# Seven products in one more column group, the last columns moved forward, and a counted order for VectorE

## Chip, core and metric

The kernel runs on one core of a Trainium2 chip. The metric is the device time of one execution in microseconds. In the text PE is TensorE (matmuls), DVE VectorE, ACT ScalarE, POOL GpSimd, and SP the engine that issues most loads.

## What is computed

A two-layer encoder trunk on 256 tokens of width 1024, all in float32. A layer is a feed-forward block, an attention block and a second feed-forward block; a norm ends it all. The change lies in the four feed-forward blocks:

```python
def rms_norm(x, g):
    y = x * lax.rsqrt(jnp.mean(x * x, axis=-1, keepdims=True) + RMS_EPS)
    return y * g
def swiglu(h, w_gate, w_up, w_down):          # 1024 -> 2816 -> 1024
    return (jax.nn.silu(h @ w_gate) * (h @ w_up)) @ w_down
for l in range(2):
    x = x + 0.5 * swiglu(rms_norm(x, ffn1_norm[l]), ffn1_w_gate[l], ffn1_w_up[l], ffn1_w_down[l])
    x = x + attention(rms_norm(x, mix_norm[l]))   # w_in, two kinds of heads, w_out
    x = x + 0.5 * swiglu(rms_norm(x, ffn2_norm[l]), ffn2_w_gate[l], ffn2_w_up[l], ffn2_w_down[l])
return rms_norm(x, final_norm)
```

## The kernel before

**Splitting.** Each float32 operand is cut in two parts of the matmul type: ACT copies it into a rounded high part and DVE subtracts that from it to get the low part. A product is then three matmuls (high by high, low by high, high by low). All weights pass once through this: a step's weights (1 MB, 512 rows by 512 columns as 128 x 4 x 512) are loaded from memory into one of six buffers called raw by a DMA that SP issues, and split in two halves (`emit_split`), each into two of the 28 slots of the pool s4. A half costs one ACT copy and one DVE subtraction of 128 x 1024. Activations are kept turned (width on the partitions), split in the same way.

**Groups of columns.** A feed-forward block's 2816 inner columns are taken in groups: 0 to 4 of 512 columns, and the last 256, here called E. In a plain group gate and up are four steps of 24 matmuls each (four chunks of 128 rows, two halves of the tokens, three matmuls). The hidden values h = silu(gate) * up are then turned on PE (eight 128 x 128 transposes) and split (`turn`), and the down projection of that group, two steps of 24 matmuls named d0.0 and d0.1 for group 0, runs one group later, into four accumulators that stay in PSUM through the block.

**Seven products.** For the groups in `SEVEN` (2, 3, 4) gate and up are one 2 x 2 block product: tokens in two halves, rows in two halves, gate and up side by side. `by_seven` makes it of seven block products of 12 matmuls each instead of eight, in the order m1, m7, p2, p3, d0, p5, p6, p4, d1 (the two down steps of the group before lie in between). Their operands are sums. On the side of the activations four sums are made once a block (`make_sums`): each is a DVE operation, an ACT copy and a DVE subtraction, from float32 copies of the normed input (`copies`, eight ACT operations). On the side of the weights (`seven`): m1 takes block a, m7 takes b+c, p2 takes d, p3 takes c, p5 takes a+b, p6 takes a+b+c, p4 takes a+b+c+d. b+c and a+b are made by accumulating DMAs that POOL issues (`gather`), once the raw buffer below is loaded, for a also split; the other two by DVE additions into raw (`plus`, two of 128 x 1024 each). DVE then combines the seven products (seven operations of 128 x 512) and multiplies gate and up (`up`, twice).

**What sets the order.** In the feed-forward blocks each engine runs its instructions in the order in which the program writes them (`keep_in_program_order`). `weights()` gives PE the next step and calls `ahead`, which writes splits up to `look` halves further on; when PE gets to the second half of a step, `part` calls it once more. `look` is 8 in a block, is brought down to 7 and 6 in groups 3 and 4 (6 throughout in the first block), and is 6 elsewhere. `ahead` also writes loads, in the order of the steps, up to ten steps on and while fewer than six raw buffers are taken; the gather of c into b goes out right behind the load of b. The block's norm statistics are written in `before(2)`, after the splits up to step 5: DVE sums, POOL's power that gives r, and DVE again. Silu needs r.

**Order of a block.** Group 0, group 1 (plain, the sums in between), groups 2 to 4 by seven, E, and the end: d4.0 with the turn of E inside, E's own down step (dE), d4.1, the residual additions (`res.add`) and the transposes for the next norm (`pair`). `attention_constants` (first block) and `final_gain` (last block) come after E. The functions that the change touches, with what calls them:

## Time and profile before

| | us |
|---|---|
| median of three runs (935.18 to 935.84) | 935.23 |
| the profiled execution: its time, and the span that the profile covers | 935.0, 933.2 |
| PE busy, matmuls / weight loads | 921.1 / 780.7 |
| DVE, ACT, POOL busy | 759.9, 566.8, 55.0 |
| granted PE clock, mean over the span | 0.999 |
| HBM read | 192.71 MB, 208 GB/s |

Matmuls are pipelined: the profile's mean duration of one (392 ns for 512 columns) is longer than the distance from one to the next. DVE's and ACT's instructions overlap a little as well, so that the distance from start to start is shorter than the duration listed. Blocks are named first to fourth feed-forward here; the second and third stand directly behind each other, and an attention block lies between first and second, and between third and fourth. The first begins at 6.14 us, group 1 of the four at 30.84, 314.08, 492.31 and 771.83.

### The profile page before, as it was taken

Reading aid. Unit: us, or ns where it says so; the run is one execution under the profiler, and the core shown is the slowest. Engines: PE = TensorE matmul, PEld = TensorE weight load, DVE = VectorE, ACT = ScalarE, POOL = GpSimd, SP = SyncE. Lnnn points to the kernel's source line nnn. Section 1 sums busy time; section 2 is a strip of 40 time slices with the busy share of each in tenths; the row PEclk is TensorE's granted clock in tenths of the full one; section 3 lists DMA queues with packets and bytes.
Section 4 is the critical chain, followed back from the end, with each engine's and each line's share of the span. In section 5 each row is a group of like instructions: output and inputs, shape, how many; then the busy total and the mean of one; then the engine's idle time right before and its main releaser. Section 6 shows DMA issues by size and latency. Waiting matters only on the chain.

```text
span 933.2 us, 12665 instructions
## 1 busy us (share of the span) xinstructions
PE 921.1 (99%) x4796; PEld 780.7 (84%) x4796; DVE 759.9 (81%) x1074; ACT 566.8 (61%) x889; POOL 55.0 (6%) x73
## 2 busy tenths in 40 slices
PE   8999999999999999999999999999999999999997
PEld 6888878799898888888888888888999888888886
DVE  6759999869866588999776799996697566799994
ACT  7837576457745657576475466565577476466561
POOL 0400000000000001000000000000000000001011
PEclk9999999999999999999999999999999999999999
DMA  9996898827335858797767597887462367597831
GB/s 334 347 233 200 251 271 270 235 97 217 131 93 178 271 135 261 191 269 271 240 236 204 140 299 203 238 283 218 144 187 91 136 213 198 145 299 203 248 113 46
DMA packets 110893, 194.58 MB, mean 208 GB/s; under 512 B 3566, under 2 KB 31280, under 8 KB 110832
## 3 DMA queue, kind: packets, MB, share of 16 engines
q1 hardware_dynamic: 96528, 166.74, 52.8%
q0 software_dynamic: 12928, 25.46, 15.4%
q10 hardware_dynamic: 1376, 1.57, 0.5%
q8 instruction: 37, 0.61, 0.3%
q14 instruction: 24, 0.20, 0.1%
HBM read 192.71 MB, written 1.05 MB: 208 GB/s over the span
## 4 chain that ended last, share of the span: by engine, by line
PE 93%; DVE 4%; issue 1%; DMA 0%; ACT 0%; POOLq 0%; POOL 0%; ACTq 0%; DVEq 0%
PE ps L50 93%; DVE w L50 3%; DVE s L50 1%; DMA xk<-in_x_dram 0%; DVE tmp L50 0%; DVE raw L50 0%; ACT w L50 0%; DVE distA L50 0%; DVE xk L50 0%; DVE distB L50 0%; POOLq L1060 0%; POOL rf L50 0%; ACTq L50 0%; DVE lsum L50 0%; DVEq L50 0%
## 5 line engine op out<-in xcount | busy, mean ns | idle before, releaser
L50 PE MATMUL ps<-w,s 128*128 128x512 f32 (+1 forms) x2754 | 641.3, 391 | 1.2 <-DVE s L50 1.1
L50 PEld LDWEIGHTS ps<-w,s 128*128 128x128 f32 x2754 | 511.3, 188 | 107.5 <-DVE s L50 1.6
L50 DVE TENSOR_TENSOR w<-raw,w 128x1024 fp32r<-128x1024 f32 (+1 forms) x440 | 460.4, 1093 | 59.3 <-ACT w L50 58.1
L50 ACT CAST w<-raw 128x1024 fp32r<-128x1024 f32 (+1 forms) x440 | 391.1, 948 | 91.9 <-DVE raw L50 69.6
L50 PE MATMUL ps<-w,q 128*128 128x512 f32 x432 | 101.9, 389 | 0.0
L50 PEld LDWEIGHTS ps<-w,q 128*128 128x128 f32 x432 | 81.1, 188 | 16.8
L50 PE MATMUL ps<-s,w 128*128 128x256 f32 x672 | 84.0, 285 | 0.0
L50 PEld LDWEIGHTS ps<-s,w 128*128 128x128 f32 x672 | 81.7, 191 | 1.1
L50 ACT ACTIVATE s<-ps,gcol 128x256 fp32r<-128x256 f32 (+1 forms) x80 | 31.5, 488 | 47.0 <-PE ps L50 47.0
L50 DVE TENSOR_TENSOR raw<-raw,raw 128x1024 f32<-128x1024 f32 x48 | 56.5, 1219 | 0.0
L50 ACT CAST s<-ps 128x512 fp32r<-128x512 f32 x48 | 26.1, 593 | 46.5 <-PE ps L50 46.5
L50 POOL DMA_DIRECT2D raw<-in_ffn_w_up_dram x24 | 31.1, 1296 | 352.9 <-DVE w L50 166.5
L50 DVE TENSOR_TENSOR s<-ps,s 128x512 fp32r<-128x512 f32 x48 | 31.0, 684 | 25.1 <-ACT s L50 25.1
L50 PE MATMUL ps<-ident,s 128*128 128x128 f32 x304 | 39.9, 274 | 0.6 <-DVE s L50 0.6
L50 PEld LDWEIGHTS ps<-ident,s 128*128 128x128 f32 x304 | 35.0, 141 | 5.9 <-DVE s L50 1.4
L50 ACT ACTIVATE tmp<-tmp,r 128x512 f32<-128x512 f32 x24 | 17.3, 722 | 34.0 <-DVE tmp L50 34.0
L50 ACT ACTIVATE s<-s,negm 128x256 f32<-128x256 f32 x64 | 31.9, 500 | 6.3 <-DVE negm L50 6.1
L50 PE MATMUL ps<-w,v 128*128 128x512 f32 x144 | 34.6, 389 | 0.0
L50 ACT CAST q<-tmp 128x512 fp32r<-128x512 f32 x20 | 12.4, 621 | 35.3 <-DVE tmp L50 35.2
L50 PEld LDWEIGHTS ps<-w,v 128*128 128x128 f32 x144 | 27.0, 188 | 5.6
L50 DVE SCALAR_TENSOR_TENSOR s<-ps,gcol,s 128x256 fp32r<-128x256 f32 x48 | 20.3, 478 | 12.5 <-ACT s L50 12.4
L50 ACT COPY tmp<-ps 128x512 f32<-128x512 f32 x24 | 14.0, 584 | 22.6 <-PE ps L50 22.5
(106 smaller groups left out, 427.0 us busy)
## 6 DMA issues: line engine op xcount, KB each, us to landing
raw<-in_ffn_w_down_dram SPq DMA_DIRECT2D x44, 1024.0 KB, 5.4
raw<-in_ffn_w_gate_dram SPq DMA_DIRECT2D x39, 1024.0 KB, 6.0
raw<-in_ffn_w_up_dram SPq DMA_DIRECT2D x39, 1024.0 KB, 5.4
raw<-in_ffn_w_up_dram POOLq DMA_DIRECT2D x24, 1024.0 KB, 10.5
raw<-in_w_in_dram SPq DMA_DIRECT2D x14, 1024.0 KB, 5.1
raw<-in_ffn_w_gate_dram SPq DMA_DIRECT2D x8, 512.0 KB, 6.4
raw<-in_ffn_w_up_dram SPq DMA_DIRECT2D x8, 512.0 KB, 7.3
raw<-in_w_in_dram SPq DMA_DIRECT2D x8, 512.0 KB, 6.3
```

Of the source, the lines that this page charges most:

```text
L50: ins = issue(*a, **k)
```

## The change

`SEVEN` is dropped: groups 1 to 4 of each block all go by seven products, and E (still plain) moves from the end of the gate and up work to the place between group 0 and group 1. Its hidden values are turned in group 1, and its down step comes first at the block's end, followed by the turn of group 4 and that group's two down steps. Two of the four sums are made inside E and two behind its hidden values; the first of them is another one, which m7 now uses.

Loads follow a list of their own (`order`), in which the next group's b and a come ahead of this group's second down step. A gather of c into b that comes due while `held` is set waits in a list; `held` is set at the program's start and at the end of each block's groups, and cleared by `stats`, which sends off what waits.

In the seven-product groups `ahead` looks no further than the step that PE takes (`take`). What DVE does beyond that is placed by a count: `clk` holds a time for PE and one for DVE, `passed` adds a step's matmuls to the first, splits and additions add 1.15 to the second, and before each combination `chain` calls `fill`, which writes splits until DVE's count reaches PE's, at most nine halves ahead. The count starts at zero for both when group 1 begins.

The attention constants move behind E's down step and the turn at the end of the first block, the final gain ahead of the last block.

```diff
@@ -155,7 +154,16 @@
-            s.behind()
+            behind.append(s.behind)
+            if not held[0]:
+                flush()
+    behind, held = [], [True]
+    def flush():
+        while behind:
+            behind.pop(0)()
     class Split:
...
@@ -209,26 +217,75 @@
+    order = []
+    fetched = set()
+    LIVE = IN_FFN + 1
+    SPLIT, ADD, PROD = 1.15, 1.15, 2.72
+    clk = dict(pe=0.0, dve=0.0)
+    ready, freed = {}, {}
+    def act_once(n):
+        i, j = divmod(at["split"], 2)
+        if at["split"] <= n and at["prep"] > i:
+            for _ in emit_split(i, j):
+                pass
+            clk["dve"] = max(clk["dve"], freed.get(at["split"] - LIVE, 0.0)) + SPLIT
+            ready[at["split"]] = clk["dve"]
+            at["split"] += 1
+            return True
+        p = at["prep"]
+        if p <= min(n // 2 + 1, len(specs) - 1) and (specs[p].moves is None or p in fetched) and \
+                (specs[p].prep is None or at["split"] >= 2 * p):
+            if specs[p].prep is not None:
+                specs[p].prep()
+                clk["dve"] += 2 * ADD * (specs[p].moves is None)
+            at["prep"] += 1
+            return True
+        return load_once()
+    def load_once():
+        k = at["dma"]
+        if k < len(order) and k < at["use"] + AHEAD and len(raws) < N_RAW:
+            for _ in emit_dma(order[k]):
+                pass
+            fetched.add(order[k])
+            at["dma"] += 1
+            return True
+        return False
     def ahead(n):
...
+        while act_once(min(n, 2 * len(specs) - 1)):
+            pass
+    def fill(until):
+        while clk["dve"] < until and at["split"] < min(2 * at["use"] + LIVE, 2 * len(specs)) and act_once(at["split"]):
+            pass
+        while load_once():
+            pass
+    def passed(i, t):
+        for h in (2 * i, 2 * i + 1):
+            clk["pe"] = max(clk["pe"], ready.get(h, 0.0)) + t / 2
+            freed[h] = clk["pe"]
+    def chain(cost, release=None):
+        r = clk["pe"] if release is None else release
+        fill(r)
+        clk["dve"] = max(clk["dve"], r) + cost
+    def take():
+        i = at["use"]
+        at["use"] += 1
+        ahead(2 * i + 1)
+        w = loaded[i]
+        w.held = True
+        return w
...
@@ -242,23 +299,28 @@
     for l in range(DEPTH):
         def ffn_specs(wg, wu, wd):
+            base = len(specs)
             down = lambda g, h: plain(wd[l], h * 512, 512, 4 * g, 4)
             for k0 in (0, 4):
                 specs.extend(plain(w[l], 0, 512, k0, 4) for w in (wg, wu))
-            for g in range(1, NGRP):
-                downs = [down(g - 1, h) for h in range(2)]
-                if g in SEVEN:
-                    specs.extend(seven(wg[l], wu[l], g * 512, downs))
-                else:
-                    specs.extend(plain(w[l], g * 512, 512, k0, 4) for w in (wg, wu) for k0 in (0, 4))
-                    specs.extend(downs)
             for k0 in (0, 4):
                 def gu_moves(t, k0=k0, ws=(wg[l], wu[l])):
                     return [(t[:, :, h * 256:h * 256 + 256], rows(w, FF - 256, 256, k0, 4)) for h, w in enumerate(ws)]
                 specs.append(Step(4, 512, gu_moves))
-            specs.append(down(NGRP - 1, 0))
+            for g in range(1, NGRP):
+                specs.extend(seven(wg[l], wu[l], g * 512, [down(g - 1, h) for h in range(2)]))
             specs.append(plain(wd[l], 0, D, 4 * NGRP, 2))
-            specs.append(down(NGRP - 1, 1))
+            specs.extend(down(NGRP - 1, h) for h in range(2))
+            a = [base + 6 + 9 * g for g in range(NGRP - 1)]
+            order.extend(range(base, base + 6))
+            order.extend((a[0] + 1, a[0]))
+            for g in range(NGRP - 1):
+                order.extend((a[g] + 2, a[g] + 3, a[g] + 4))
+                if g + 1 < NGRP - 1:
+                    order.extend((a[g + 1] + 1, a[g + 1]))
+                order.append(a[g] + 8)
+            order.extend(range(a[-1] + 9, len(specs)))
         ffn_specs(g1, u1, d1)
         wi = w_in[l]
...
@@ -346,11 +409,11 @@
                 self.sm.append(sm)
                 return v
+            make(t1, t0, ALU.subtract)
+            yield
             s1 = make(b1, t1, ALU.subtract)
             yield
             s2 = make(s1, t0, ALU.add)
-            yield
-            make(t1, t0, ALU.subtract)
             yield
             make(b0, s2, ALU.subtract)
             yield
...
+            held[0] = False
+            flush()
         def spread(self, sl):
...
@@ -605,36 +669,59 @@
                 dve.tensor_tensor(o, x, y, op=op)
                 return o
+            def product(xo):
+                w = take()
+                acc = prod(xo, w)
+                passed(w.i, PROD)
+                return acc
+            def down_(h):
+                w = take()
+                down(hT, g - 1, h, w)
+                passed(w.i, 2 * PROD)
             m1, m7 = flat(), flat()
-            act.copy(m1, prod(norm.quarter(0, 0), weights()))
-            act.copy(m7, prod(norm.summed(2), weights(held=True)))
-            hT = turn(h, 2)
-            p2 = prod(norm.quarter(0, 1), weights())
+            act.copy(m1, product(norm.quarter(0, 0)))
+            fill(clk["pe"])
+            act.copy(m7, product(norm.summed(0)))
+            hs = []
+            clk["pe"] = max(clk["pe"], clk.get("up", 0.0))
+            for i in range(1 if g == 1 else 2):
+                clk["pe"] += 0.45
+                chain(0.65, clk["pe"] + 0.6)
+                hs.extend(turn(h, (i,)))
+            if g > 1:
+                hT = hs
+            p2 = product(norm.quarter(0, 1))
+            chain(0.65)
             g0 = put(flat(), p2, m1, ALU.add)
-            p3 = prod(norm.summed(3), weights())
             silu(g0, g0, 0)
-            down(hT, g - 1, 0, weights())
+            p3 = product(norm.summed(3))
+            down_(0)
             h = blk(F32)
-            p5 = prod(norm.summed(0), weights())
-            late = g == max(SEVEN)
-            p6 = prod(norm.summed(1), weights(look[0] - 5 if late else 0, late))
+            p5 = product(norm.summed(1))
+            p6 = product(norm.summed(2))
+            chain(1.3)
             u2 = put(flat(), p6, m1, ALU.subtract)
             u3 = put(m7, m7, u2, ALU.add)
-            p4 = prod(norm.quarter(1, 1), weights(look[0] - 4 if late else 0, late))
+            p4 = product(norm.quarter(1, 1))
+            chain(0.65)
             g1 = put(m1, p4, u3, ALU.subtract)
-            w = weights(look[0] - 3 if late else 0)
             silu(g1, g1, 1)
+            chain(2.7)
             put(u3, u3, p5, ALU.subtract)
             put(u2, u2, p5, ALU.subtract)
             put(u2, u2, p3, ALU.add)
             up(h, u2, g0, 0)
+            chain(0.7)
             up(h, u3, g1, 1)
-            down(hT, g - 1, 1, w)
-            return h
+            clk["up"] = clk["dve"]
+            down_(1)
+            return hs, h
         def turn(hs, n):
             out_ = []
-            for i in range(n):
+            for i in (range(n) if isinstance(n, int) else n):
                 sl = halves(bank())
                 for c in range(2):
                     for t in range(2):
...
         h = hidden(g, us)
...
+        norm.copies()
+        sums = norm.make_sums()
         gu = [bank(), bank()]
         tokens(gu, norm.xs, weights(), 0)
         hT = turn(h, 2)
+        for _ in range(2):
+            next(sums)
         tokens(gu, norm.xs, weights(), 4)
         h = hidden(gate([b[:, 0:256] for b in gu]), [b[:, 256:512] for b in gu])
+        for _ in sums:
+            pass
+        clk.update(pe=0.0, dve=0.0, up=0.0)
+        ready.clear()
+        freed.clear()
+        hE, h = by_seven(hT, h, 1)
+        for n in range(2, NGRP):
+            h = by_seven(None, h, n)[1]
+        held[0] = True
+        look[0] = IN_MIX
+        return accs, hE, lambda: turn(h, 2)
+    BY_TOKENS = [(k, t) for t in range(2) for k in range(2)]
+    ALL = [(k, t) for k in range(4) for t in range(2)]
+    G4 = 4 * (NGRP - 1)
+    def tail(accs, hE, w, h, last=-1):
+        tokens(accs, [None] * (2 * NGRP) + hE, w, 4 * NGRP, last=last, order=BY_TOKENS, h=h)
+    def group(accs, hT, w, order, c=slice(None), first=0):
+        tokens(accs, [None] * (2 * (NGRP - 1)) + hT, w, G4, first=first, last=G4 + 3, order=order, cols=c)
+    def ffn_close(parts, nxt, aside=None):
+        accs, hE, turn_ = parts
+        res = Residual(nxt, accs)
+        we = weights(3, True)
+        for h in range(2):
+            tail(accs[h], hE, we, h)
+        hT = turn_()
         if aside is not None:
             aside()
...
+        group(accs[0], hT, weights(), ALL)
         for t in range(2):
             res.add(0, t)
...
+        w = weights()
+        group(accs[1], hT, w, ALL[:4])
...
         for j in range(2):
             nxt.pair(j)
         res.squares(0)
...
+        group(accs[1], hT, w, ALL[4:])
         for t in range(2):
             res.add(1, t)
         nxt.late = res.late
...
-        parts = ffn(norm, attention_constants, take_x) if l == 0 else ffn(norm)
+        parts = ffn(norm, take_x if l == 0 else None)
         norm_m = Norm(16 + l * 8, False)
-        ffn_close(parts, norm_m)
+        ffn_close(parts, norm_m, attention_constants if l == 0 else None)
         norm2 = Norm(32 + l * 8)
         mix(l, norm_m, norm2)
-        parts = ffn(norm2, final_gain if final else None, final=final)
+        if final:
+            final_gain()
+        parts = ffn(norm2)
         if not final:
             norm = Norm((l + 1) * 8)
             ffn_close(parts, norm)
...
+    accs, hE, turn_ = parts
+    we = weights(3, True)
+    tail(accs[0], hE, we, 0)
+    tail(accs[1], hE, we, 1, (-1, FC - 1))
     dve.tensor_tensor(xk[:, 1, 512:D], xk[:, 1, 512:D], accs[1][1], op=ALU.add)
-    group(1, [(k, 0) for k in range(2)])
-    tail(0)
+    hT = turn_()
+    group(accs[0], hT, weights(), ALL)
...
+    w = weights()
+    group(accs[1], hT, w, [(k, 0) for k in range(4)])
...
+        group([None, acc], hT, w, [(k, 1) for k in range(4)], slice(c, c + 256), G4)
         close(1, 512 + c, 256, acc)
```

More of the change, by code (lines that the diff above doesn't have):

```diff
@@ L30 @@
 IN_FFN, IN_MIX = 8, 6
-SEVEN = (2, 3, 4)
 @with_exitstack
@@ L283, in trunk @@
             specs.append(Step(2, D, o_moves))
+        order.extend(range(mixed, len(specs)))
         fine.update(range(mixed + 2, len(specs)))
@@ L565, in late, with ffn @@
                 self.nxt.stats()
-    def ffn(norm, aside=None, before=None, final=False):
+    def ffn(norm, before=None):
         def silu(out_, acc, t):
@@ L649, in down @@
         def down(hT, g, h, w):
-            tokens(accs[h], [None] * (2 * g) + hT, w, 4 * g, last=(FC - 1, G4 - 1) if final and h else FC - 1)
+            tokens(accs[h], [None] * (2 * g) + hT, w, 4 * g, last=-1)
         gs, us = [bank(), bank()], [bank(), bank()]
@@ L725, in ffn_close @@
-    def ffn_close(parts, nxt):
-        group, tail = ffn_end(parts, (FC - 1, G4 + 3))
-        res = Residual(nxt, parts[0])
-        group(1, [(0, t) for t in range(2)])
-        tail(0)
+        group(accs[0], hT, weights(), ALL)
         for t in range(2):
             res.add(0, t)
-        tail(1)
-        ahead(2 * at["use"] - 2 + look[0])
-        group(1, [(1, t) for t in range(2)])
+        w = weights()
+        group(accs[1], hT, w, ALL[:4])
         for j in range(2):
@@ L737, in ffn_close @@
         res.squares(0)
-        group(1, [(2, t) for t in range(2)])
-        group(1, [(3, t) for t in range(2)])
+        group(accs[1], hT, w, ALL[4:])
         for t in range(2):
```

71 lines of the change are left out of this document (2 added, 69 removed).

## The prediction

> **What bounds the kernel now.** First the busy times of the page, then the chain of work that ended last, in order of time.
>
> ```profile
> PE 921.1 (99%) x4796; PEld 780.7 (84%) x4796; DVE 759.9 (81%) x1074; ACT 566.8 (61%) x889; POOL 55.0 (6%) x73
> ```
> ```profile
> 9.12 122.98 PE ps L50 x554
> ...
> 142.11 2.27 DVE raw L50 x2
> 144.38 0.60 DVE tmp L50
> 144.98 2.27 DVE w L50 x2
> ...
> 179.75 742.84 PE ps L50 x3983
> ```
> TensorE (PE) carries the chain, except from 132 to 180 us: there, in the first feed-forward, VectorE (DVE) does. So I cut the second feed-forward into its stages (busy time of each engine by stretch: groups 2, 3, 4, then the last 256 columns, called E).
>
> ```profile
> core 0: us, PE busy (x) PEld busy (x) DVE busy (x) ACT busy (x) POOL busy (x), PEclk, DMA share, GB/s
> 347.65:378.46 30.81, 30.81 (x141) 25.61 (x140) 26.61 (x27) 18.02 (x21) 2.57 (x2) 1.00 0.85 234
> 378.46:409.31 30.85, 30.85 (x142) 25.61 (x140) 30.37 (x32) 19.44 (x23) 2.57 (x2) 1.00 0.80 240
> 409.31:440.12 30.81, 30.81 (x141) 25.60 (x140) 30.67 (x34) 20.25 (x24) 0.00 (x0) 1.00 0.81 247
> 440.12:451.93 11.81, 11.81 (x58) 9.84 (x56) 11.77 (x13) 6.93 (x9) 0.00 (x0) 1.00 0.82 290
> ```
> After the length of a stretch come PE, the weight loads, DVE, ACT and POOL, each with its instructions. In groups 3 and 4 PE and DVE are both full. Read split by split in the timeline, the first weight half of m1 is ready 16.7 us before PE takes it in group 2, 8.2 in group 3, 6.4 in group 4, and 3.6 at E; for p4 it is 4.6, 3.3 and 1.4. A seven-product group uses up lead, and the plain group 1 ahead of it fills it (DVE busy 23.9 of 33.6 us there). In the first feed-forward the lead is gone at p4 of group 3, and that part takes 159.25 us (30.84 to 190.09) where the second takes 155.58: 3.7 us lost, 1.1 of them behind the attention constants.
>
> **Part 1, seven products in group 1.** Twelve matmuls go per feed-forward. Rows for their price, with DVE's:
>
> ```profile
> 401.15 11.04 PE L50 MATMUL ps<-w,s 128*128 128x512 f32 x48
> 412.03 2.89 PE L50 MATMUL ps<-w,q 128*128 128x512 f32 x12
> 413.89 3.49 DVE L50 TENSOR_TENSOR w<-raw,w 128x1024 fp32r<-128x1024 f32 x3
> 406.51 2.36 DVE L50 TENSOR_TENSOR w<-raw,w 128x1024 fp32r<-128x1024 f32 x2
> ```
> (11.04-2.89)/36 = 0.226 us a matmul, 2.72 for twelve, all on the path: **-10.9** for four. DVE gets six splits (3.49-2.36 = 1.13 each), four adds (1.13) and seven combinations (0.62): 15.6 us per feed-forward. POOL gets two accumulating loads (1.30 us of issue each; its queue is 15.4% of the span for 24, so 6.0 us of all 16 DMA engines each). A group then needs six loads at 3.1 and two at 6.0, 30.6 us of DMA, under the 32 that DVE takes; I price that at nothing, and SP issues as many loads as before.
>
> **Part 2, what four such groups need of DVE.** I wrote out the order that the new count gives. When PE starts m1 of group 1, the program has put eight halves (m1, m7, p2, p3) ahead of it; the next, the first half of the down projection d0, stands behind the sums. From it to the first half of p4 in group 4 DVE does 61 splits and 16 adds (77 x 1.13 = 87.0), 29 operations at 0.62 (18.0) and six at 0.66 (4.0): 109.0. The same prices give 60.1 for the stretch from 369.08 to 430.60 of the second feed-forward, where DVE never rests and which took 61.5; so 111.5. PE gets to that p4 3 x 30.85 - 0.4 (half a turn less) + 22.65 = 114.8 after m1. DVE can thus begin on d0 **3.3 us** after PE begins group 1; each microsecond later is one PE waits. (With 32.2 a group, as in the first feed-forward, it would be 4.3; with 32.65, 2.6.)
>
> **Part 3, when it does begin.** E now runs just ahead of group 1. Set its start to 0; PE ends it at 5.44 + 0.80 + 5.44 = 11.7. The order of DVE and ACT here is: group 0's two ups, the xg copies, two splits, the turn, two sums, two splits, E's silu and ups, two more sums, then ACT's copy of m1 and d0. One sum is a subtraction, an ACT copy and a subtraction, each waiting for the last, with nothing to slip between:
>
> ```profile
> 327.42 0.68 DVE L50 TENSOR_TENSOR tmp<-s,s 128x512 f32<-128x512 f32 x1
> 328.14 0.62 ACT L50 CAST q<-tmp 128x512 fp32r<-128x512 f32 x1 [0.91 <-DVE tmp L50]
> ...
> 328.80 0.69 DVE L50 TENSOR_TENSOR q<-tmp,q 128x512 fp32r<-128x512 f32 x1 [0.69 <-ACT q L50]
> ```
> 2.05 us a sum. Turn 8.0, two sums 12.0, splits to 14.7, ups to 15.5, two sums 19.6, copy and cast of d0 (0.55, 1.05) 20.4: d0 is 8.7 late. Were nothing else late, silu alone (PE's end 11.9, then ups 13.3, sums, copy, cast 17.8) gives 6.1.
>
> What is late beyond that is m7, whose raw must have had its accumulating load. The change holds these until the norm's statistics; m7's two splits stand in front of group 0's ups, so the chain starts when the load lands: m7's casts 2.1, copies 3.0, two casts 2.0, the turn 1.1 + 1.6, two sums 4.1, splits and ups 3.6, two sums 4.1, copy and cast 0.9 (half beside the last sum): 22.4, less 11.7, so d0 is (landing - start of E) + 10.8 late. POOL rows:
>
> ```profile
> 305.34 0.70 POOL L50 TENSOR_TENSOR r<-ms,mhalf 128x2 f32<-128x2 f32 x1 [42.00 <-DVE ms L50]
> 311.38 1.33 POOL L50 DMA_DIRECT2D raw<-in_ffn_w_up_dram  x1 [5.34 <-ACT tmp L50]
> ```
> Such a load lands 8.3 us (332.40 to 340.68) to 14.4 us (43.64 to 58.03) after its issue.
> - First feed-forward: statistics at 28.2, landing 36.5 to 42.6, E at 30.84: 16.5 to 22.6 late. Its second held gather makes POOL wait for a raw and pushes the constants and the third gather back. I take 18, nearer the lower end, as fewer loads are out by then.
> - Third (follows the second directly, held too): statistics at 484.3, E at 492.3, landing +0.3 to +4: 11 to 15; I take 12.
> - Second and fourth: nothing is held, but group 2's gather is now issued ahead of r and waits for its raw, as at 311.38; r moves from 305.3 to 312.7 and with it silu and the casts behind it: 8.7 to 11.3; I take 10.
>
> Less 3.3 each: 14.7 + 6.7 + 8.7 + 6.7 = **+36.8** of PE waiting. From it goes the 2.6 us (3.7 less 1.1) that the first feed-forward loses in its groups already: **-2.6**.
>
> **Part 4, the end.** The turn of group 4 now stands directly ahead of its first use. In the old order six matmuls or a whole step lay between. PE waits for ACT's copy (0.59) and DVE's low part (0.68), less the 0.4 of the second four transposes: 0.9 x 4 = **+3.6** (bounds 1.6 and 4.8). The first half's residual adds stand behind five or six look-ahead splits (5.7 to 6.8 us) that DVE, with no lead left, now does late; the constants (3.5 us) moved in front of them too. PE has 5.4 + 2.7 us of cover: between 0 and 4.8 in all; **+2.4**. Moving E itself is the same matmuls, and the output's end is as before. The final gain now comes ahead of the fourth feed-forward: POOL does its 2.9 us there early, ahead of r, and it holds one of the 28 slots throughout, as the constants' two do in the first; with a lead this short DVE doesn't reach that limit, so nothing.
>
> [...] Every row shows PEclk 1.00, and no PE pause after the first microseconds exceeds 1.1 us; in the first feed-forward I expect one of about 7 us, as the turn waits for group 0's ups. [...]
>
> **Sum**: -10.9 + 36.8 - 2.6 + 3.6 + 2.4 = +29.3 on the profiled execution's own 935.0 (0.2 under the median): **964 us**.
>
> **Rivals.**
> - *The lead holds* (faster). Groups 2 to 4 of before start with DVE already on d1 when PE begins m1, and never stop PE in the last three feed-forwards. If the sums and ups slip in so that d0 is at most 3.3 us late everywhere, -10.9 and the 2.6 count in full, with 0 to 3.6 at the end: 922 to 925. It decides at d0 5.7 late, where 4 x 2.4 of waiting and 3.6 of turns use up the 13.5. Against it: silu, ups and two sums stand in one queue behind E's last matmul, 6.1 at the least.
> - *Only E's chain counts* (gathers land in time, no delay of r): d0 6.1 to 8.7 late, 4 x 2.8 to 5.4 of waiting and 3.6 of turns against 13.5, so +1 to +12: 936 to 947. For it: accumulating loads did land in 8.3 us where little else moved.
> - *DMA too* becomes late: in the first feed-forward the gather of a+b behind the constants lands at 62 to 70 where DVE is due at 65 (waits on POOL add up: raw at 42, constants 12.3, issue 1.3, landing), and 30.6 us of DMA a group leaves little room: 5 more in the first, 2 to 3 in each other: 975 to 985.
>
> **Chances.** Forecast 0.60 (952 to 975); E's chain alone 0.18; DMA 0.11; the lead holds 0.11. With the bounds: low, each d0 at its early end and 0.7 more lead a feed-forward, 952; high, late ends, 983. The range takes in most of E's chain: **944 to 984**. About 0.2% (1.9 us) is what a measurement can tell here. Faster 0.10 (the lead holds, without its balanced end), same 0.03, slower 0.87.
>
> **What would show it.** In groups 1 to 4 DVE full and PE pausing at p4, p6 and the down steps; each feed-forward's groups about 7 to 9 us longer than 4 x 30.8, the first one 15. The first d0 split 9 to 12 us after m1's first matmul. In the first, a PE pause of several us before the first turn after E. POOL's r 7 us later against E in the second and fourth. I am wrong if d0 is split within 4 us of m1, or if DVE rests in groups 2 to 4 while PE runs without a pause.

## The result, and the profile after

The changed kernel takes **1009.32 us** (median of 4 runs, 1007.26 to 1010.71), the kernel before beside it 935.54 us (4 runs, 935.18 to 935.86): ratio **1.079**, 95% interval 1.077 to 1.081. The profiled execution of the changed kernel took 1007.26 us, its span 1005.2 us. The forecast was 964 us (944 to 984): slower, as forecast, but by 74 us, not 29.

On the page, PE does less work than before (4742 instructions: the 48 matmuls fewer of the forecast, and six because E's down step in the last block is no longer cut in two half widths) and is busy 20 us longer; its granted clock is 0.982 in the mean, where it was 0.999.

```profile
PE 941.2 (94%) x4742; PEld 776.9 (77%) x4742; DVE 825.4 (82%) x1142; ACT 594.0 (59%) x921; POOL 64.5 (6%) x81
```

The four feed-forwards, from their first weight matmul to the first one of what follows (the last to the end of the span), took 211.8, 191.9, 194.8 and 198.3 us; before 184.0, 178.2, 178.2 and 184.0. That is 72.4 us more, and the attention blocks took the same time (101.2 and 101.3 us). So all of it lies in the feed-forwards, over 13 us in each and 28 in the first.

Next, busy time by stretch in the second feed-forward: E, then groups 1, 2, 3 and 4 (columns as in the prediction's view).

```profile
341.63:353.43 11.80, 11.80 (x57) 9.84 (x56) 7.42 (x11) 6.28 (x12) 0.00 (x0) 1.00 0.96 219
353.43:386.10 32.67, 31.15 (x137) 24.85 (x136) 28.53 (x31) 20.01 (x25) 1.28 (x1) 1.00 0.46 160
386.10:419.48 33.38, 31.48 (x140) 25.56 (x141) 31.51 (x33) 19.93 (x23) 2.57 (x2) 1.00 0.87 247
419.48:454.10 34.62, 32.77 (x141) 26.60 (x140) 34.34 (x38) 19.80 (x23) 2.60 (x2) 0.95 0.89 250
454.10:485.27 31.17, 27.05 (x118) 20.63 (x116) 25.07 (x25) 19.20 (x22) 0.00 (x0) 1.00 0.55 158
```

The first three seven-product groups take 32.7, 33.4 and 34.6 us where groups 3 and 4 before took 30.8. The last stretch ends where PE begins the group's second down step, so its 31.2 us lack 24 matmuls, 5.4 us: with them it is 36.6, the longest of the four. The third number after the length is what I had not expected: DVE is not full. In group 4 it works 25.1 of 31.2 us while PE waits too. From the first half of d0 to the first half of p4 of group 4 DVE rests 10.0 us in this feed-forward, and 10.1 to 10.7 in the others. The page's groups name what it rests for (busy us and mean ns of one, then idle time just before them and what ended it):

```profile
L49 DVE TENSOR_TENSOR w<-raw,w 128x1024 fp32r<-128x1024 f32 (+1 forms) x464 | 486.6, 1101 | 88.1 <-ACT w L49 86.9
L49 ACT ACTIVATE tmp<-tmp,r 128x512 f32<-128x512 f32 x32 | 23.2, 724 | 125.1 <-DVE tmp L49 125.1
L49 ACT COPY tmp<-ps 128x512 f32<-128x512 f32 x32 | 18.7, 585 | 25.7 <-PE ps L49 24.5 <-issue 1.1
```

The silus (second line) had much less idle time in the kernel before, for 24 instructions:

```profile
L50 ACT ACTIVATE tmp<-tmp,r 128x512 f32<-128x512 f32 x24 | 17.3, 722 | 34.0 <-DVE tmp L50 34.0
```

Now ACT stands 125 us in front of 32 of them. ACT is only 59% busy, but the weight casts that DVE's splits need stand behind them in its queue. Two places of the second feed-forward in the timeline, first a silu in group 2, then m1's copy in group 4:

```profile
403.24 0.69 DVE L49 TENSOR_TENSOR tmp<-ps,tmp 128x512 f32<-128x512 f32 x1
...
403.96 0.72 ACT L49 ACTIVATE tmp<-tmp,r 128x512 f32<-128x512 f32 x1 [5.54 <-DVE tmp L49]
404.59 1.98 ACT L49 CAST w<-raw 128x1024 fp32r<-128x1024 f32 x2
...
405.66 2.36 DVE L49 TENSOR_TENSOR w<-raw,w 128x1024 fp32r<-128x1024 f32 x2 [1.73 <-ACT w L49]
...
457.07 0.59 ACT L49 COPY tmp<-ps 128x512 f32<-128x512 f32 x1 [4.70 <-PE ps L49]
457.56 3.90 ACT L49 CAST w<-raw 128x1024 fp32r<-128x1024 f32 x4
458.63 3.50 DVE L49 TENSOR_TENSOR w<-raw,w 128x1024 fp32r<-128x1024 f32 x3 [3.54 <-ACT w L49]
...
458.65 0.73 PE L49 MATMUL ps<-w,q 128*128 128x512 f32 x2 [1.67 <-ACT w L49]
```

Read from the end of each. DVE waits for a cast; the cast follows at once on a silu or a copy; that one had stood 5.54 or 4.70 us for DVE's combination or PE's product. Those microseconds are time enough for four or five casts (four took 3.90 us). DVE could not split, so PE in its turn waited (1.67 us for a cast in the second place), and with it the products for which ACT's next operations wait. In the second place ACT is idle for 4.70 us while four casts stand behind that copy, and none of them went ahead of it.

In the first feed-forward there is more, all around E:

```profile
27.98 1.47 POOL L49 DMA_DIRECT2D raw<-in_ffn_w_up_dram  x1
...
33.93 7.35 PE L49 MATMUL ps<-w,s 128*128 128x512 f32 x24 [3.30 <-ACT tmp L49]
41.46 1.99 ACT L49 CAST w<-raw 128x1024 fp32r<-128x1024 f32 x2 [7.00 <-DMA raw<-in_ffn_w_up_dram]
...
45.70 2.32 PE L49 MATMUL ps<-ident,s 128*128 128x128 f32 x8 [4.43 <-DVE s L49]
```

The accumulating load of m7's raw, issued at 27.98 us, has landed at 41.4; m7's casts wait 7.00 us for it and hold what stands behind; PE waits 3.30 us at the start of E and 4.43 us for the turn in it.

### The profile page after: what moved, and what is told of

Its sections match the earlier page's. It is cut to its first block, busy times and chain, and to the rows that moved or that the text cites. A ratio compares the mean times of both kernels' runs of the same rounds, so it can differ in the third digit from the quotient of the medians.

```text
span 1005.2 us, 12734 instructions
## 1 busy us (share of the span) xinstructions
PE 941.2 (94%) x4742; PEld 776.9 (77%) x4742; DVE 825.4 (82%) x1142; ACT 594.0 (59%) x921; POOL 64.5 (6%) x81
## 5 line engine op out<-in xcount | busy, mean ns | idle before, releaser
L49 PE MATMUL ps<-w,s 128*128 128x512 f32 x2508 | 606.3, 398 | 31.6 <-DVE s L49 15.0
L49 PEld LDWEIGHTS ps<-w,s 128*128 128x128 f32 x2508 | 470.8, 191 | 144.4 <-DVE s L49 19.6
L49 DVE TENSOR_TENSOR w<-raw,w 128x1024 fp32r<-128x1024 f32 (+1 forms) x464 | 486.6, 1101 | 88.1 <-ACT w L49 86.9
L49 ACT CAST w<-raw 128x1024 fp32r<-128x1024 f32 (+1 forms) x464 | 413.2, 953 | 83.1 <-DVE raw L49 60.7
L49 PE MATMUL ps<-w,q 128*128 128x512 f32 x576 | 141.3, 396 | 11.0 <-ACT w L49 6.6
L49 PEld LDWEIGHTS ps<-w,q 128*128 128x128 f32 x576 | 107.7, 189 | 39.7 <-ACT w L49 9.7
L49 ACT ACTIVATE tmp<-tmp,r 128x512 f32<-128x512 f32 x32 | 23.2, 724 | 125.1 <-DVE tmp L49 125.1
L49 DVE TENSOR_TENSOR raw<-raw,raw 128x1024 f32<-128x1024 f32 x64 | 75.4, 1220 | 0.0
L49 POOL DMA_DIRECT2D raw<-in_ffn_w_up_dram x32 | 41.6, 1317 | 468.9 <-DVE w L49 400.9
L49 PE MATMUL ps<-w,v 128*128 128x512 f32 x192 | 46.5, 390 | 0.2 <-DVE v L49 0.2
L49 DVE TENSOR_TENSOR s<-ps,s 128x512 fp32r<-128x512 f32 x48 | 31.0, 685 | 14.3 <-ACT s L49 14.3
L49 ACT COPY tmp<-ps 128x512 f32<-128x512 f32 x32 | 18.7, 585 | 25.7 <-PE ps L49 24.5
L49 DVE TENSOR_TENSOR tmp<-ps,tmp 128x512 f32<-128x512 f32 x48 | 32.9, 686 | 0.0
```

Source lines behind the costliest of these rows:

```text
L49: ins = issue(*a, **k)
```

## The experiments

Theory O (order): DVE could do its work in time, but ACT's casts stand behind ACT operations that wait for DVE or PE. Rival W (work): four seven-product groups in a row are too much for DVE, and its rest only mirrors waits that would come anyway. Theory H (head start): d0 is late because of the sums around E. The table has the time of one execution (the median for before, late_m7 and late_start; for the changed kernel the profiled one, 1007.3 us, from which the gains below are counted and which is the lowest of its four, 3.5 us apart), the four feed-forwards, and of the second one three readings: when d0's first half is ready after m1's first matmul, the time from there to the same of p4 in group 4, and DVE's rest in that stretch.

```
kernel         time    1st    2nd    3rd    4th   d0 after m1  d0 to p4  DVE rests
before         935.5  184.0  178.2  178.2  184.0       -          -         -
changed       1007.3  211.8  191.9  194.8  198.3      9.5       119.9     10.0
act_late       967.9  202.6  181.4  185.6  187.8      9.0       109.9      0.5
old_order     1003.8  208.4  192.9  195.1  196.9      9.0       117.2      7.5
no_adds        962.3  198.8  180.7  184.7  187.6      9.5       103.8     12.7
sums_g0       1003.1  209.0  193.0  191.2  199.1      5.7       120.2     10.3
late_now       963.3  201.4  182.3  181.4  187.8      9.0       110.0      0.5
late_sums      946.3  196.2  177.3  178.2  183.7      2.9       111.1      1.5
late_all       942.7  191.4  177.3  177.3  183.8      2.9       111.1      1.5
old_act_late   968.9  197.7  183.5  187.3  189.7      9.0       109.7      0.5
late_m7        945.6  194.2  177.3  177.3  183.7      2.9       111.1      1.5
silu_late      992.9  208.9  185.9  192.1  195.3      9.5       113.9      4.2
copies_late    988.6  207.9  186.8  189.9  193.2      9.0       115.4      5.7
late_start     939.2  187.6  177.3  177.3  183.8      2.9       111.1      1.5
```

**act_late: ACT's waiting operations behind the casts**

```
-            act.copy(m1, product(norm.quarter(0, 0)))
+            acc = product(norm.quarter(0, 0))
             fill(clk["pe"])
-            act.copy(m7, product(norm.summed(0)))
+            act.copy(m1, acc)
+            acc = product(norm.summed(0))
...
                 chain(0.65, clk["pe"] + 0.6)
+                if i == 0:
+                    act.copy(m7, acc)
...
             g0 = put(flat(), p2, m1, ALU.add)
-            silu(g0, g0, 0)
...
             p6 = product(norm.summed(2))
+            silu(g0, g0, 0)
             chain(1.3)
...
-            silu(g1, g1, 1)
             chain(2.7)
+            silu(g1, g1, 1)
```

> Edit: in each seven-product group the ACT operations that wait for PE or DVE (the copies of m1 and m7, both silus) are emitted behind the weight casts that the count puts out at that point, instead of ahead of them. Theory O (the order starves DVE: the 9.5 us per feed-forward that DVE rests between d0 and p4 of group 4 are casts queued on ACT behind an operation that waits): ACT's idle time in front of the silus falls from 125 us to under 50, DVE's rest from 10.0 us to 3 or less per feed-forward, time 970 to 985 against 1007.3. Rival W (four seven-product groups in a row are too much work for DVE, the rest only mirrors waits that come anyway): the rest moves to other operations, time 1002 to 1010.

967.9 us, 2 us under the range of theory O: **39.4 us back**, from the place of four ACT operations per group; the work is the same. The second feed-forward from d0 to p4 of group 4, by stretch, and the page's groups:

```profile
353.48:463.40 109.92, 108.07 (x482) 87.56 (x480) 109.42 (x113) 70.60 (x83) 6.46 (x5) 1.00 0.83 240
```
```profile
L49 DVE TENSOR_TENSOR w<-raw,w 128x1024 fp32r<-128x1024 f32 (+1 forms) x464 | 486.1, 1099 | 49.1 <-ACT w L49 47.4
L49 ACT ACTIVATE tmp<-tmp,r 128x512 f32<-128x512 f32 x32 | 23.1, 723 | 71.6 <-DVE tmp L49 71.6
L49 ACT COPY tmp<-ps 128x512 f32<-128x512 f32 x32 | 18.5, 577 | 3.5 <-PE ps L49 3.5
```

DVE is busy 109.4 of 109.9 us. Its waits for casts fall from 86.9 to 47.4 us, by 39.5: the gain. ACT's idle before the silus fell to 71.6 us, where I had expected under 50: it still waits there, only nothing that DVE needs stands behind.

**silu_late and copies_late: the halves of that edit.** silu_late moves only the two silus, copies_late only the two copies.

> Edit: of act_late only the two silus of each seven-product group are moved down; the copies of m1 and m7 stay where the change put them. Theory O (a silu waits for DVE's combination, which waits for PE's product, and holds every cast behind it): at least three quarters of act_late's 40 us, 968 to 978, DVE's rest from 10 us to under 3 per feed-forward. Rival (the copies, which wait for PE's m1 and m7, hold as much): 985 to 998.

> Edit: of act_late only the copies of m1 and m7 are moved down; the silus stay where the change put them. act_late gave back 39.4 us, silu_late 14.4 of them. Theory (each waiting operation costs what stands behind it, the two shares add): the other 25, 978 to 987. Rival (they overlap: a cast let past one is held by the next, so either alone gives little and it takes both): 988 to 1000.

silu_late gives 14.4 us back, copies_late 18.7, together 33.1 of the 39.4. Theory O's three quarters for the silus missed by far: I had named the operation with the longest idle time on the page, and the copies, whose own idle was 25.7 us, held about as much. The copies alone end at 988.6 us, by a hair in the range of "it takes both"; by the sum most of it adds up, and 6.3 us take both edits. From the pages of silu_late, then copies_late:

```profile
L49 ACT COPY tmp<-ps 128x512 f32<-128x512 f32 x32 | 18.7, 584 | 34.4 <-PE ps L49 27.9 <-issue 6.5
```
```profile
L49 ACT ACTIVATE tmp<-tmp,r 128x512 f32<-128x512 f32 x32 | 23.2, 725 | 134.2 <-DVE tmp L49 134.2
```

With the silus moved, the copies wait 34.4 us instead of 25.7; with the copies moved, the silus wait 134.2 instead of 125.1: part of what one lets past, the other holds.

Which of the two holds more is not shown. Each is a single execution, and the clock is mixed in: in silu_late PE's granted clock falls to half for 3.41 us twice in the groups of the first, third and fourth feed-forward, but never in those of the second. From d0 to p4 these three take 116.8, 117.0 and 116.8 us with 7.3 to 7.4 us of rest, the second 113.9 with 4.2, so its row in the table is the exception. In copies_late the clock never falls there, and all four take 115.3 to 115.4 us. Where the clock holds, moving the silus thus saves 6.0 us of the changed kernel's 119.9 (which itself holds one such fall) and moving the copies 4.5; by the time of the whole kernel it is the other way round.

**old_order and old_act_late: the count out of use.** Each step asks for the halves up to eight ahead; in old_act_late the edit of act_late is made too.

```
-                w = take()
+                w = weights(0, held)
...
     def fill(until):
 
+        return
...
     def chain(cost, release=None):
 
+        return
```

> Edit: group 1 by seven products, E ahead of it, the sums, the loads and the held gathers stay as changed, but the count is out of use: every step asks for the weight halves up to eight ahead, as the program did before, whatever waits. Theory O: the count, which knows DVE and PE only and starts both at zero, is what makes ACT and DVE wait for each other; without it DVE needs 110.4 us instead of 119.9 from d0 to p4 of group 4, time 965 to 980. Rival W: the same DVE work in another order, 1000 to 1012.

> Edit: as act_late (copies and silus moved down), but without the count: every step asks for the halves up to eight ahead. It tells whether the count is worth or costs anything once ACT's waiting operations are out of the casts' way. Theory O1 (only the place of ACT's operations matters): 964 to 974, as act_late's 967.9. Theory O2 (the count's order of VectorE's work is needed too): 978 or more, DVE's rest 4 us or more per feed-forward between d0 and p4 of group 4.

1003.8 us, in the range of rival W, and 968.9 us, as theory O1 has it. So it is not the count that starves DVE: without it, with ACT's operations where the change put them, DVE still rests 7.5 us, and with them moved, 0.5 us with or without the count. That part of theory O, which blamed the count, falls; the place of ACT's operations stays (theory O1).

**before_late: the same move in the kernel before.** The copies of m1 and m7 and the first silu are moved down in the same way.

> Edit: in the kernel before, the copies of m1 and m7 and the first silu of each seven-product group are moved down in the same way. Theory (a cast that waits behind a silu costs nothing as long as the splits are ahead of PE, as in the kernel before, so the same order of ACT only began to cost when the lead was used up): no change in three feed-forwards, some of the first one's 3.7 us at most, 931 to 937. Rival (the order costs the kernel before as well): 925 or less.

934.9 us beside 935.4, where the kernel before spread from 934.9 to 935.9 in seven runs. A cast behind a waiting silu cost nothing here, while the splits were ahead of PE; the trap had no price as long as there was a lead.

**no_adds: less work for DVE**

```
-                Step(4, 512, None, prep=plus(c, a), src=a, free=[c]),
-                Step(4, 512, None, prep=plus(d, a), src=a, free=[a, d]),
+                Step(4, 512, None, src=a, free=[c]),
+                Step(4, 512, None, src=a, free=[a, d]),
```

> Leaves out the two additions of weight blocks per group that VectorE makes ahead of p6 and p4 (p5, p6 and p4 then multiply by unfinished sums); all else as changed, loads and matmuls too. It prices the amount of DVE work: 16 half-adds of 1.13 us, 18.1 us less per feed-forward. Rival W (amount of work): DVE's end moves by all of it until PE is the bound, so 4 x 14 to 18 us less, 935 to 952. Theory O (order): DVE is shorter but its casts still wait behind silus, which wait for PE; of the 72 us less than 55 come back, 952 to 975, and DVE's rest per feed-forward grows from 10 to 15 us or more.

962.3 us, 45 us less for 72 us less work, in the range of theory O and 10 us outside that of W. DVE's rest grew to 12.7 us, short of the 15 or more that theory O expected. Taking 72 us of work from DVE thus buys 5.6 us more than the order alone did in act_late, with all the work kept. The two are not added: either one, less work or a cleared queue, gives back more than half of the loss.

**sums_g0: the sums in group 0**

```
         before(2)
+        norm.copies()
+        for _ in norm.make_sums():
+            pass
         tokens(gs, norm.xs, weights(), 4)
...
-        norm.copies()
-
-        sums = norm.make_sums()
...
-        for _ in range(2):
-            next(sums)
...
-        for _ in sums:
-            pass
```

> Edit: the copies of the turned input and all four sums of its quarters are made in group 0, behind the norm's operands, instead of around E. Theory H (the head start: d0 is late by the two sums behind E's ups and by two ahead of them): d0's first half is ready 3 to 6 us after m1 in the second and fourth feed-forward instead of 9.5, 4 to 8 us sooner in the first and third, each microsecond one that PE waits: 16 to 28 less, 980 to 992 against 1007.3. Rival: the sums push back the splits of E and of m1 and m7 by the same 8 us, nothing gained, 1002 to 1012.

1003.1 us: mostly the rival. d0 came 3.8 us sooner after m1, but E took 16.4 instead of 11.8 us: four sums one after the other, each with a wait of DVE for ACT (0.69 us) and of ACT for DVE (1.36), push back the silu and the ups of group 0, PE waits 2.3 us for the turn, and the granted clock behind that wait is 0.84.

**late_sums: sums in group 0 without waits between, and act_late**

```
+            v0 = add(t1, t0, ALU.subtract)
+            s1 = add(b1, t1, ALU.subtract)
+            s2 = add(s1, t0, ALU.add)
+            vs = [v0, s1, s2, add(b0, s2, ALU.subtract)]
+            for v in vs:
...
+                act.copy(sm[:, :, 0:P], v)
+                self.sm.append(sm)
+            for v, sm in zip(vs, self.sm):
+                dve.tensor_tensor(sm[:, :, P:S], v, f(sm[:, :, 0:P]), op=ALU.subtract)
```

> Edit: as act_late, and the sums are made in group 0, the four differences and sums first, then their four copies on ScalarE, then the four subtractions, so that no engine waits between. With ACT's waits out of the casts' way the lateness of d0 should be all that is left of the 2nd and 4th feed-forward's loss. Theory H (DVE rests 11.2 us in group 0 of the second feed-forward, the sums fit there): d0 4 to 5 us earlier from the start of each feed-forward, each 4 to 5 us shorter, 948 to 955 against 967.9. Rival (in group 0 the casts on ACT and the buffers set the pace, so E's weights come late by what d0 gains, as in sums_g0, where E took 16.4 us instead of 11.8): 962 to 970.

946.3 us, 21.6 less than act_late and a little more than theory H gave, once the sums wait for nothing and E keeps its 11.8 us. d0 is ready 2.9 us after m1, and in the second to fourth feed-forward PE goes from m1 of group 1 to the last down step of group 3 in 117.5 us, the time without any pause. At 9.0 us it had taken 121.4. By that, d0's first half may be ready 9.0 - 3.9 = 5.1 us after m1's start (the forecast's 3.3 for the start of its split is 4.4 for its end).

**late_now, late_all, late_m7, late_start: the first and third feed-forward**

late_now is act_late with the gathers issued at once (`held` false from the start). late_all is late_sums and late_now, with the attention constants behind the first residual adds. late_m7 adds a shorter look-ahead in the first feed-forward, so that m7's casts stand behind group 0's ups (`weights(2, True)`, `weights(2, True)`, `weights(3, True)` in the three steps ahead of the turn). late_start is late_m7 with the first feed-forward's gathers held again and GpSimd's constants moved behind group 1.

> Edit: as act_late, and the gathers are issued with their loads again, none is held until the norm's statistics. It prices the hold, which the first and third feed-forward have (m7's raw waits for its accumulating load). Theory (the hold is what makes those two longer): the third loses its pause in E, 185.6 to 181.4 us like the second, the first 202.6 to 195 or less; 955 to 964 against 967.9. Rival (GpSimd then waits for a raw ahead of the norm's power, the silu of group 0 comes late as it does in the second and fourth, and nothing is gained or some lost): 966 to 976.

> Edit: act_late, late_sums and late_now together, and the attention constants put behind the residual adds of the first half instead of ahead of d4's products in the first feed-forward. If head start, hold and constants each cost what the theories say, they add up: 967.9 less 16 to 20 (sums), less 8 to 12 (hold), less 2 to 4 (constants): 932 to 942, about the time before. Rival (the amount of DVE work in four seven-product groups is the floor, as DVE rests 0.5 us in 110 there): not under 950.

> Edit: as late_all, and in the first feed-forward the weights are asked for less far ahead in the last three steps before the turn, so that m7's casts and splits (they wait until 41.4 us for the accumulating load) stand behind group 0's silu and ups instead of ahead of them. In late_all PE waited 9.9 us there, the clock fell to 0.78, and the first feed-forward took 191.4 us; the other three took 177.3, 177.3 and 175.9. Theory (that pause is m7's raw in front of the ups, and nothing else there is late): the pause goes, the first feed-forward takes 179 to 184, the whole 930 to 936: at or under the time before. Rival (the loads of the start are late anyway: PE waits for E's or m7's weights a step further on): 939 to 945.

> Edit: as late_m7, and in the first feed-forward only the start is changed: the gathers of it are held until the norm's statistics again (later ones not), and GpSimd's making of the constants is moved from the statistics to behind group 1. In late_m7 the first feed-forward took 194.2 us: PE waited 4.1 us for the turn, behind a power that GpSimd made late, as it stood behind a gather, and ACT waited 9.2 us for p6's accumulating load, issued at 52.0 us behind the constants. Theory (those two places of GpSimd's queue are what the first feed-forward loses): both waits go, it takes 179 to 185, the whole 930 to 937. Rival (the loads of the start, at a DMA share above 1 until 42 us, land late whoever issues them): 940 to 946.

- late_now: 963.3 us. The third feed-forward is 4.1 us shorter, as expected, the first only 1.2, and the second 0.9 longer. (The expectation has r late in the second and fourth feed-forward; it is not, as the next section shows.)
- late_all: 942.7 us, 0.7 us outside what I gave and under the 950 of the rival. Three feed-forwards are now at or under those before (177.3, 177.3, 183.8); the first is 7.4 us longer, and the first attention block 2.4 (103.7 us; it has 101.2 in late_sums and late_now, where the constants were not moved). The first feed-forward's timeline, ACT, then PE:

```profile
41.62 3.88 ACT L49 CAST w<-raw 128x1024 fp32r<-128x1024 f32 x4 [3.36 <-DMA raw<-in_ffn_w_up_dram]
...
45.87 2.32 PE L49 MATMUL ps<-ident,s 128*128 128x128 f32 x8 [9.76 <-DVE s L49]
```

  The casts of m7 stand ahead of the ups again, and PE waits 9.76 us.
- late_m7: 945.6 us (ratio to before 1.011, interval 1.010 to 1.013), the rival. The pause ahead of the turn shrank to 4.0 us, and ACT waited a step later, for p6's gather, which GpSimd issued at 52 us behind the constants:

```profile
51.99 2.68 POOL L49 DMA_DIRECT2D raw<-in_ffn_w_up_dram  x2
...
61.39 1.05 ACT L49 CAST w<-raw 128x1024 fp32r<-128x1024 f32 x1 [9.19 <-DMA raw<-in_ffn_w_up_dram]
```
- late_start: **939.2 us** (5 runs, 938.4 to 939.5; before 935.8; ratio 1.0035, interval 1.002 to 1.005). Between theory and rival: the first feed-forward took 187.6 us. That gather is now issued at 39.5 us and ACT waits 1.34 us for it, but GpSimd's next one still waits 8.34 us for a raw, and m7's casts 2.42 us for their load. The DMA share is full to 55 us (1.08 and 1.10; stretches of late_start, columns as above):

```profile
30.50:42.00 11.50, 9.98 (x48) 7.99 (x47) 8.14 (x12) 6.75 (x10) 1.30 (x1) 1.00 1.08 300
42.00:55.00 13.00, 12.29 (x56) 9.79 (x55) 11.63 (x12) 11.47 (x15) 1.28 (x1) 1.00 1.10 274
```

No version of this plan came out under the kernel before. Against it, late_start gains 0.9, 0.9 and 0.2 us in the second to fourth feed-forward and loses 3.6 in the first and 2.4 in the attention block behind it. Whether the first one's rest is DMA alone was not settled further.

## Why the prediction was right or wrong, point by point

**The step that failed is Part 2: "what four such groups need of DVE", 111.5 us, by a stretch "where DVE never rests".** That sum was right as work: with ACT's queue cleared, DVE takes 109.9 us from d0's first half ready to p4's, and the forecast says 110.4 (111.5 less the 1.1 of the first split itself). But in the changed kernel it takes 119.8 to 120.5 us. I took the price from a stretch of the kernel before in which DVE had a lead (it rests 0.6 of 61.5 us there), so a cast that came late held nobody up. The change adds waits on ACT's queue (a silu and a copy directly behind the product they need, ahead of casts), and I did not ask what stands behind each of them. I had the row: the silus' 34.0 us of idle before. It was harmless there, as before_late shows, and I left it out.

**Part 3 came near in its numbers, by its mechanism only in the first and third feed-forward.** Forecast for the start of d0's split, from where m1 would stand without pauses: 18, 10, 12, 10 us late. Measured in the changed kernel: 20.5, 8.3, 11.3, 8.3 us. In the first and third it is the held load, as forecast: ACT waits 7.00 and 6.03 us for it ahead of m7's casts. In the second and fourth I had r about 7 us late behind a gather, and that did not happen: POOL begins r 13.9 us after the feed-forward's first matmul in both kernels (305.34 and 291.42 before; 332.83 and 318.96, 820.84 and 806.91 now), and the next gathers are issued after it, at 336.32 and 824.31. What is left is the chain of E alone, forecast at 6.1 to 8.7 us. That 10 was near 8.3 is luck, and the sign that I had named for it, r 7 us later, failed.

The waits of PE that follow from d0's lateness, with DVE's work as forecast, can be read in act_late, summed over E and group 0 too (time from m1 to the last down step of group 3, less 117.5, plus the pauses ahead): 17.7 + 3.9 + 8.0 + 3.7 = 33.3 us, forecast 36.8. In the changed kernel the same sum is 27.0 + 14.3 + 17.3 + 14.2 = 72.8. The difference, 39.5, is act_late's gain. Off in size were the limit (0.7 us more than forecast) and the first feed-forward, 2.5 us later than forecast. Two slips moved nothing: the terms of m7's chain add up to 22.5, not 22.4, and the slowest accumulating load before took 15.6 us (49.16 to 64.75), not 14.4.

**Part 1** (-10.9) holds: without pauses PE takes 117.5 us from m1 of group 1 to the last down step of group 3, as 48 matmuls fewer give, and late_sums reaches it.

**Part 4** was too small: +6.0 forecast. A feed-forward's length less before's, less the waits just listed, plus the 2.72 us of twelve matmuls leaves what the end costs: 191.9 - 178.2 - 14.3 + 2.7 = 2.0 us in the second, 2.0 in the third, 2.8 in the fourth, and 7.3 in the first (there without the 3.7 us that the kernel before loses), 14.1 together. Of the first's, 4.5 us went when late_all moved the constants (30.6 to 26.1 us from the last down step of group 3 on), but 2.5 came back in the attention block.

The sum with the measured terms: -10.9 + 72.8 - 3.7 + 14.1 = +72.3, which is what the profiled executions differ by; as the ends are what was left over, it closes by construction. Of the 43.0 us over the forecast's +29.3 the waits make 36.0 and the ends 8.1, less 1.1 for the constants in the kernel before that I had kept out of its loss.

**The rivals.** "The lead holds" needed d0 at most 3.3 us late; it was 8.3 or more. "Only E's chain" has what came in the second and fourth feed-forward, but not in the other two, and its time, 936 to 947, lacks DVE's longer stretch as the forecast does. "DMA too" was present in the first feed-forward (7.00 us of ACT, 8.45 us of GpSimd for a load), but it is not what made the other three long: late_sums has the same loads, and its groups run without pauses there. None of my rivals had ACT's order in it. The sign that would prove me wrong, "if DVE rests in groups 2 to 4 while PE runs without a pause", was half of what came: DVE rested, and PE paused with it.

**The clock** has no term in the sum, and it cost something. The forecast pause of about 7 us came as two, 3.30 and 4.43, and the clock fell to half five times in the groups as well, which I had not forecast. What that cost is only an estimate. From d0 to p4, one such fall in act_late makes 0.5 us (110.4 in its first feed-forward, 109.9 in the others), two in silu_late 3 us (116.8 against 113.9): 0.5 to 1.5 us each, some 3 to 7 us for the five. As act_late has one of them left, 2 to 6 of its 39.4 us came by way of the clock.

## What to carry to other kernels

An engine that is only 59% busy can hold up all others: before you price the work of the busiest engine, write out the queue of the one that feeds it, and for each operation in it that waits, ask what stands behind. A stretch in which an engine never rests proves its speed only for the lead that it had there; once the lead is gone, an order that cost nothing (before_late) cost 39 us. And the idle time in front of an operation is not what it costs: moving the silus, with 125.1 us of it, gave 14.4 us back, moving the copies, with 25.7, gave 18.7.

## What the runs showed of the hardware

PE's granted clock fell to half at pauses of 3.30 and 4.43 us, and at one of two of 1.85. Two stretches of the changed kernel, behind the pauses of 3.30 and 4.43 us (columns as above; the sixth number after the length, 0.59 and 0.50, is PE's granted clock):

```profile
33.93:38.00 4.07, 4.07 (x11) 3.24 (x12) 0.00 (x0) 0.52 (x1) 0.00 (x0) 0.59 1.10 260
...
45.70:49.00 3.30, 3.18 (x11) 2.69 (x12) 2.17 (x3) 3.30 (x6) 0.85 (x2) 0.50 0.95 325
```

The trace records the clock at half for 3.41 us from 34.70 on, behind the first, and for 6.83 us from 44.94 on, the last 0.76 us of the second and behind it; eight transposes took 2.32 us there, where they take 1.04 us at full clock. In late_start, whose pauses at that place are at most 1.25 us, the clock stayed at 1.00 throughout E. And two equal pauses in the groups of the second feed-forward, PE's timeline:

```profile
400.51 5.51 PE L49 MATMUL ps<-w,s 128*128 128x512 f32 x23 [1.85 <-DVE s L49]
...
433.53 7.13 PE L49 MATMUL ps<-w,s 128*128 128x512 f32 x23 [1.85 <-DVE s L49]
```

After 1.85 us of waiting the same 23 matmuls took 5.51 us in one place and 7.13 us in the other, where the granted clock of the two microseconds from 435.50 is 0.51.

The same trace tells the two apart. Its stretches of half clock up to the last matmul last 3.41 us or twice that, and they begin whole multiples of 3.413 us apart (34.70, 44.94, 102.97, 160.99, 212.19, 434.06 us and so on). I went through the trace in pieces of that length, counted from there. The pause that ends at 433.53 lies within one piece: from 430.65 to 434.06 PE is busy for 1.55 of 3.41 us, and the next piece has clock 0.50. The one that ends at 400.51 lies across two: from 396.51 PE is busy for 2.15 us, from 399.93 for 2.83, and the clock stays at 1.00. In this execution, past its first 12 us and short of its last 8, eight pieces have PE at work for less than 0.47 of their length (0.00 to 0.46), and each is followed by one at half clock; of the pieces with 0.57 or more of work at full clock none is.
